# One buffer and one 1 MB transfer in place of two halves for two of three weight pieces

## The chip, the cores and the metric

The kernel runs on one core of one Trainium2 chip. The metric is the device time of one execution, in microseconds. The kernel before took 734.4 us (median of three runs, 733.27 to 735.97).

## The reference

Two decoder layers over 256 tokens of width 1024, in float32:

```
for l in 0, 1:
    x = LN(alpha*x + mixer_l(x))   # l=0: differential attention beside retention; l=1: forgetting attention
    h = LN(alpha*x + moe(x))       # router: 4 groups of 4 experts, top 2 of 16, FF = 512, silu(g)*u
    x = h + gate(h, p[l])          # per-layer input embedding, width 256
```

Every expert has three matrices (g and u of 1024 x 512, d of 512 x 1024). All 16 experts are computed for both layers.

## The kernel before

**Weights as pieces.** All weights lie in DRAM as 236 pieces of 1 MB, each 128 partitions by 2048 float32. `PLAN` lists them in the order of use: for layer 0, 16 pieces of the mixer (0 to 15), then 96 of experts and two "pp" pieces (half the size) of the MoE (16 to 113) and 4 "pg" pieces of the gate; layer 1 follows in the same way from 118, with its mixer up to 133 and its MoE from 134. A matrix g, u or d of one expert is two pieces, written here as d(l, e, fh): layer, expert, half.

**Buffers.** `fetch` takes the next piece of PLAN, asks the pool `wp` for room, and starts the transfers on SP's DMA queue (`dma_start`, line 289). The pool has 36 buffers of 128 x 1024 (512 KB, a row of 4 KB in each partition), so a piece has two of them and comes in two transfers. A buffer's next transfer is held back until the last reader of what lay in it is done. A few pieces (`PLACES`) go to other memory, among them three "late" ones and the ones in slots per layer: they come in one transfer of 1 MB. The pieces d(l, 10, 1) and d(l, 11, 1) come in transfers of 256 KB, so that the first of their rows can start early. SP executes its instructions strictly in order: a transfer that waits for its buffer holds back all that stand behind it. A transfer also waits for the one eight places ahead of it to have landed, since eight semaphores go round.

**The MoE.** Experts run in 7 units: pairs, one unit of four (12 to 15), and last the pair (10, 11), called LAST. For a unit, PE computes g and u (line 1309), transposes the product, and runs the down rows (line 1339). Matmul rows of a pair have 64 partitions each and two run side by side; those of the unit of four have 32.

**The end of layer 1.** In PLAN the tail of the last MoE reads d(1, 10, 0), d(1, 11, 0) (227, 228), three pg pieces (229 to 231, `EARLY`), d(1, 10, 1), d(1, 11, 1) (232, 233), the pp piece 234 and the pg piece 235. `early` (lines 401 to 408) splits the three EARLY pieces into high and low parts, which lie in 12 more buffers of the pool (tiles "wf"). After the last down rows come a layer norm, and the gate with its pg and pp weights (line 1553).

The order of instructions on each engine is set ahead by a scheduler from the program and the buffers' release; it needn't be the order in which the code asks.

Of the kernel before, what the change touches and what calls it, by code (L numbers as in the profile page):

```python
# [10 lines left out]
F32 = mybir.dt.float32  # L11
FR = mybir.dt.float32r
# [19 lines left out]
DEPTH = 2  # L32
NBUF = 18
CUT = 2
NSPL = 4
PPAT = 5

# [33 lines left out]
def plan():  # L71
    out = []
    for l in range(DEPTH):
        if l == 0:
            cols = [0, 512, 1536, 1024, 2048, 2560]
            out += [("ein", c, kh) for c in cols for kh in range(2)]
        else:
            def qk(g):
                return [("oqk", g, kh) for kh in range(2)]

            def v(h):
                return [("ov", h, kh) for kh in range(2)]
            out += qk(0) + v(0) + qk(1) + v(1) + qk(2) + qk(3)
        out += [("wo", l, kh, nh) for kh in range(2) for nh in range(2)]
        out += moe_steps(l)
        out += [k for k in [("pg", l, nh, kh) for nh in range(2) for kh in range(2)] if k not in EARLY]
    return out


PLAN = plan()  # L90
# [140 lines left out]
def trunk(ctx: ExitStack, tc, w, xT_d, pT_d, prm_d, rows_d, rb_d, cst_d, e_d, dt_d, out):  # L231
# [4 lines left out]
    big = ctx.enter_context(tc.tile_pool(name="big", bufs=1))  # L236
    wp = ctx.enter_context(tc.tile_pool(name="wp", bufs=NBUF * CUT))
    wsp = ctx.enter_context(tc.tile_pool(name="wsp", bufs=NSPL))
    small = ctx.enter_context(tc.tile_pool(name="small", bufs=2))
# [9 lines left out]

    def room(n=4):  # L250

        return [wp.tile([128, 2048 // CUT], F32, name="wt", tag="wt") for _ in range(n * CUT // 4)]

    def quarters(t):
        return [x[:, j:j + 512] for x in t for j in range(0, x.shape[-1], 512)]
# [3 lines left out]
    def source(key, c):  # L259

        if key[0] in ("g", "u", "d") and key[2] >= FIXED:
            l = key[1]
            of = w[(l * NE + FIXED) * 6:(l + 1) * NE * 6].rearrange("(x j) p c -> x j p c", j=6)
            if callable(ranked[l]):
                ranked[l] = ranked[l]()
            return of[bass.ds(ranked[l][key[2] - FIXED], 1), "gud".index(key[0]) * 2 + key[3], :, c]
        return w[AT[key], :, c]

    def fetch(n=1):
        for _ in range(n):  # L270
            i = pos[0]
            if i >= NCHUNK:
                return
            place = PLACE.get(i)
            if place == "split":
                t = [wsp.tile([128, 512], F32, name="wt", tag=g) for g in ("whi", "wlo") for _ in range(2)]
            elif place is None:
                t = room(2 if PLAN[i][0] == "pp" else 4)
            elif place == "late":
                t = [late[0].tile([128, 2048], F32, name="wt", tag="late")]  # L280
            else:
                t = [slot(XSLOT[PLAN[i][1]][place], "wt", shape=(128, 2048))]
            c = 0
            for part in t:
                n = part.shape[-1]

                m = 512 if PLAN[i][0] == "d" and PLAN[i][2] in UNITS[LAST] and PLAN[i][3] else n
                for j in range(0, n, m):
                    nc.sync.dma_start(out=part[:, j:j + m], in_=source(PLAN[i], slice(c + j, c + j + m)))
                c += n  # L290
            t = quarters(t)
            ahead[PLAN[i]] = t
            pos[0] += 1

    def take(key, drop=True):

        while key not in ahead:
            fetch()
        return ahead.pop(key) if drop else ahead[key]
# [5 lines left out]
    def slot(i, name, dt=F32, shape=(128, 8, S)):  # L305

        return big.tile(list(shape), dt, name=name, tag=f"s{i}")
# [18 lines left out]
    for k in range(8):  # L326
# [3 lines left out]
        c = (k % 4) * 512  # L330
# [19 lines left out]
    wf = prm[:, P_WF:P_WF + 256].rearrange("p (k e) -> p k e", k=8)  # L350
# [29 lines left out]
    def split(hi, lo, src, after=None, eng=None, first=None):  # L380
        with tc.issue_after(first.ins) if first else ExitStack():
            i = ACT.activation(hi, src, AF.Copy)  # L382
        with tc.issue_after(after.ins) if after else ExitStack():
            return i, (eng or DVE).tensor_tensor(lo, src, hi, op=OP.subtract)  # L384
# [10 lines left out]

    def prepare(keys, n=NSPL):

        for i in range(n):
            part(keys[i // 4], i % 4)

    def early(keys, after):

        for key in keys:
            for j in range(4):
                t = wp.tile([128, 2048 // CUT], FR, name="wf", tag="wt")
                hi, lo = t[:, 0:512], t[:, 512:1024]
                after = split(hi, lo, take(key, drop=j == 3)[j], after[1], None, after[0])
                parted[key, j] = hi, lo
        return after
# [219 lines left out]
    def even(x2, y2, acc):  # L629
        with ExitStack() as es:  # L630
# [23 lines left out]
            heads_T(kaT, 512, 1.0)  # L654
            centred(0)
            fetch(2)
            nc.sync.dma_start(out=scr, in_=bt)
            fetch()
# [965 lines left out]
```

## Time and profile before

| | before |
|---|---|
| median of three runs | 734.4 us |
| profiled execution, its own time | 737.25 us |
| its span | 735.4 us |
| PE busy | 711.4 us (97%) |
| DMA moved | 250.82 MB, mean 341 GB/s |
| mean granted TensorE clock | 0.995 |

The profiled execution took 2.85 us more than the median of the runs; sums of durations are held against its own span. The span is cut by the program into the mixer of layer 0 (to about 132 us), its MoE (to about 335), the mixer of layer 1 (to about 494), its MoE (to about 702), and the last norm and gate. "Busy" of PE contains rows that stretch because operands come late, so 97% is not a share of useful work.

### The profile page before, as it was taken

What the parts mean: (1) busy time and instruction counts of PE and PEld (TensorE: products, weight loads), DVE (VectorE), ACT (ScalarE), POOL (GpSimd) and SP (SyncE); (2) the same over time, 40 slices, a digit from 0 to 9 for tenths busy, and PEclk for the clock granted to TensorE, in tenths of its full rate; (3) what the DMA queues carried; (4) which work ended last, traced back from release to release, by engine and by line L of the source; (5) the groups of instructions that cost most, each with busy time, mean ns of one, the idle gap of its engine ahead of it and who ended that gap; (6) DMA issues with size and microseconds to landing.
All of it is one profiled execution on the core that took longest, in us unless ns stands there. A gap on an engine that the chain in (4) does not pass through costs nothing.

```text
span 735.4 us, 11580 instructions
## 1 busy us (share of the span) xinstructions
PE 711.4 (97%) x4126; PEld 427.8 (58%) x4126; DVE 320.7 (44%) x805; ACT 242.4 (33%) x507; POOL 45.8 (6%) x44
## 2 busy tenths in 40 slices
PE   6999999999999998999999999989999999999897
PEld 6977887434335334338989898764353343343267
DVE  6687776412103103019857666672031121120585
ACT  5557656201102001006667566561010110110441
POOL 3000111000000000004000000010000000000036
PEclk9999999999999999999999999999999999999899
DMA  8999977999999999999997337559999999999901
GB/s 287 354 410 408 371 263 261 322 389 415 410 408 414 408 407 410 408 377 401 409 408 301 128 141 282 185 189 333 412 413 409 412 411 408 406 410 408 391 4 58
DMA packets 70397, 250.82 MB, mean 341 GB/s; under 512 B 7835, under 2 KB 9408, under 8 KB 67648
## 3 DMA queue, kind: packets, MB, share of 16 engines
q1 hardware_dynamic: 70176, 249.51, 87.6%
q8 instruction: 34, 0.56, 0.3%
q0 software_dynamic: 160, 0.52, 0.2%
q14 instruction: 27, 0.22, 0.1%
HBM read 248.95 MB, written 1.05 MB: 340 GB/s over the span
## 4 chain that ended last, share of the span: by engine, by line
PE 76%; DMA 18%; DVE 3%; ACT 2%; issue 1%; POOL 0%; SPq 0%; DVEq 0%; ACTq 0%; POOLq 0%
PE w L1309 21%; DMA wt<-in_w_dram 18%; PE acc L420 13%; PE acc L434 13%; PE w L1339 11%; PE w L1247 3%; PE acc L1553 2%; PE acc L1359 2%; PE w L962 1%; PE w L1008 1%; PE w L1322 1%; PE w L1553 1%; DVE lnst L458 1%; PE w L622 1%; PE w L782 1%
## 5 line engine op out<-in xcount | busy, mean ns | idle before, releaser
L1309 PE MATMUL w<-wt,xg 128*64 128x512 f32 (+1 forms) x1024 | 202.7, 595 | 2.3 <-DMA wt<-in_w_dram 1.3
L1309 PEld LDWEIGHTS w<-wt,xg 128*64 128x64 f32 (+1 forms) x1024 | 63.7, 130 | 122.7 <-issue 112.6
L1339 PE MATMUL w<-wt,aT 128*64 128x512 f32 (+1 forms) x512 | 123.5, 604 | 3.7 <-DMA wt<-in_w_dram 3.5
L384 DVE TENSOR_TENSOR wlo<-wt,whi 128x512 fp32r<-128x512 f32 x145 | 106.3, 749 | 43.2 <-ACT whi L382 36.6
L382 ACT ACTIVATE whi<-wt 128x512 fp32r<-128x512 f32 x148 | 91.0, 629 | 65.6 <-PE acc L434 27.5
L1339 PEld LDWEIGHTS w<-wt,aT 128*64 128x64 f32 (+1 forms) x512 | 38.4, 132 | 80.1 <-issue 68.5
L1350 ACT ACTIVATE whi<-w,gg 128x512 fp32r<-128x512 f32 x28 | 19.3, 688 | 157.6 <-PE w L1339 150.4
L1316 DVE TENSOR_TENSOR a<-a,w 128x512 f32<-128x512 f32 x14 | 9.6, 688 | 127.2 <-PE w L1309 127.2
L434 PE MATMUL acc<-xh,whi 128*128 128x256 f32 x192 | 51.5, 293 | 5.6 <-ACT whi L382 5.6
L434 PE MATMUL acc<-xh,wlo 128*128 128x256 f32 x192 | 51.1, 290 | 0.0
L1315 ACT ACTIVATE a<-w 128x512 f32<-128x512 f32 x14 | 8.4, 597 | 123.0 <-PE w L1274 57.5
L1351 DVE SCALAR_TENSOR_TENSOR wlo<-w,gg,whi 128x512 fp32r<-128x512 f32 x28 | 20.6, 746 | 64.7 <-ACT whi L1350 64.4
L434 PEld LDWEIGHTS acc<-xh,whi 128*128 128x128 f32 x192 | 37.9, 199 | 6.8 <-ACT whi L382 6.6
L434 PEld LDWEIGHTS acc<-xh,wlo 128*128 128x128 f32 x192 | 38.0, 198 | 0.4 <-DVE wlo L384 0.2
L420 PE MATMUL acc<-whi,xh 128*128 128x512 f32 x96 | 38.1, 396 | 0.0
L420 PE MATMUL acc<-whi,xl 128*128 128x512 f32 x96 | 38.0, 396 | 0.0
L434 PE MATMUL acc<-xl,whi 128*128 128x256 f32 x192 | 37.5, 288 | 0.0
L420 PE MATMUL acc<-wlo,xh 128*128 128x512 f32 x96 | 37.1, 390 | 0.0
L1257 ACT ACTIVATE xg<-w,prm 128x256 f32<-128x256 f32 (+1 forms) x32 | 15.5, 533 | 62.9 <-PE w L1247 62.9
L1247 PE MATMUL w<-sel,n 128*128 128x256 f16 (+1 forms) x256 | 28.1, 260 | 2.6 <-ACT xg L1257 1.8
L434 PEld LDWEIGHTS acc<-xl,whi 128*128 128x128 f32 x192 | 29.9, 198 | 0.0
L1324 DVE COPY aT<-w 128x512 f32<-128x512 f32 x14 | 9.7, 690 | 45.7 <-PE w L1339 32.3
(318 smaller groups left out, 988.0 us busy)
## 6 DMA issues: line engine op xcount, KB each, us to landing
wt<-in_w_dram SPq DMA_DIRECT2D x406, 512.0 KB, 10.1
wt<-in_w_dram SPq DMA_DIRECT2D x21, 1024.0 KB, 9.3
wt<-in_w_dram SPq DMA_DIRECT2D x40, 256.0 KB, 5.8
x<-in_xT_dram SPq DMA_DIRECT2D x3, 256.0 KB, 5.4
dt<-in_dt_dram SPq DMA_DIRECT2D x1, 512.0 KB
tmp<-scr SPq DMA_DIRECT2D x1, 512.0 KB, 7.1
pT<-in_pT_dram POOLq DMA_DIRECT2D x2, 256.0 KB, 6.8
out_dram<-wt SPq DMA_DIRECT2D x2, 256.0 KB, 2.7
```

The costliest lines, as they stand in the source:

```text
L382: i = ACT.activation(hi, src, AF.Copy)
L384: return i, (eng or DVE).tensor_tensor(lo, src, hi, op=OP.subtract)
L420: PE.matmul(o, lhsT=wa[p], rhs=wb[q], start=start and i == 0, stop=stop and i == 2, skip_group_check=True)
L434: m = PE.matmul(outs[b], lhsT=ws[kk][i % 2][:, b * 128:(b + 1) * 128], rhs=x2[i // 2][:, kk, :], start=kk == 0 and b in first and i == 0, ...
L1247: PE.matmul(os[kb][:, b, :], lhsT=n2[j][:, tt, k * 128:(k + 1) * 128], rhs=sel[:, tt, 0:n], start=b == 0 and i == 0, stop=i == 3, skip_gro ...
L1257: ACT.activation(xt[:, k, 0:n], o[:, b, :], AF.Identity, bias=be, scale=g)
L1309: PE.matmul(o[m * i:m * i + m, :], lhsT=xg[p // 2][:, k, c:c + m], rhs=ws[i, k // 4][k % 4], start=k == 0, stop=k == 7)
L1339: PE.matmul(ob[nh][m * i:m * i + m, :], lhsT=aT[p][:, f, m * i:m * i + m], rhs=ws[i, f // 2][2 * (f % 2) + nh], start=f == 0, stop=f == 3)
L1350: last[:] = (ACT.activation(yh, ob[nh], AF.Copy, scale=gg), DVE.scalar_tensor_tensor(yl, ob[nh], gg, yh, op0=OP.mult, op1=OP.subtract))
L1351: DVE.scalar_tensor_tensor(yl, ob[nh], gg, yh, op0=OP.mult, op1=OP.subtract))
L1359: j = PE.matmul(acc[tt][nh], lhsT=sT[p // 2][:, p % 2, tt * 128:(tt + 1) * 128], rhs=y2[nh][i], start=False, stop=p == LAST and i == 1, sk ...
L1553: PE.matmul(gs[j], lhsT=h22[i % 2][:, kk, tt * 128:(tt + 1) * 128], rhs=ws[kk][i // 2][:, units[nh][j][1]], start=kk == 0 and i == 0, stop ...
```

## The change

Of the 36 half buffers, 24 are put together to 12 whole buffers of 128 x 2048 (1 MB, rows of 8 KB, tag "wb"); 12 halves stay. The memory is the same. A counter sends the pieces that go to the pool, but for the pp ones, to a half pair, a whole, a whole, and so on. A piece in a whole buffer comes in one transfer. The three EARLY pieces' parts lie in 6 whole buffers where they took 12 halves.

```diff
 NBUF = 18
 CUT = 2
+WHOLE = 12
...
     def room(n=4):
-        return [wp.tile([128, 2048 // CUT], F32, name="wt", tag="wt") for _ in range(n * CUT // 4)]
+        return [wp.tile([128, 2048 // CUT], F32, name="wt", tag="wt", bufs=(NBUF - WHOLE) * CUT) for _ in range(n * CUT // 4)]
+
+    def whole_room(name="wt", dt=F32):
+        return wp.tile([128, 2048], dt, name=name, tag="wb", bufs=WHOLE)
+
+    turn = [0]
...
+            elif place is None and PLAN[i][0] == "pp":
+                t = room(2)
             elif place is None:
-                t = room(2 if PLAN[i][0] == "pp" else 4)
+                turn[0] += 1
+                t = [whole_room()] if turn[0] * WHOLE % NBUF < WHOLE else room()
...
             for j in range(4):
-                t = wp.tile([128, 2048 // CUT], FR, name="wf", tag="wt")
-                hi, lo = t[:, 0:512], t[:, 512:1024]
+                if j % 2 == 0:
+                    t = whole_room("wf", FR)
+                hi, lo = [t[:, c:c + 512] for c in range(j % 2 * 1024, j % 2 * 1024 + 1024, 512)]
```

The order of SP's transfers at the end of the last MoE, before. Of the tiles, 6320 and 6321 are piece 231 (pg), 6335 and 6336 piece 232, 6341 and 6342 piece 233, 6381 the pp piece 234, 6458 and 6459 the pg piece 235. An "ISA" row is a wait for a buffer.

```order
L289 DMA wt_6320<-in_w_dram 128x1024
L289 DMA wt_6321<-in_w_dram 128x1024
L289 ISA
L289 DMA wt_6335<-in_w_dram 128x512
L289 ISA
L289 DMA wt_6335<-in_w_dram 128x512
L289 ISA
L289 DMA wt_6336<-in_w_dram 128x512
...
L289 DMA wt_6381<-in_w_dram 128x1024
L289 DMA wt_6458<-in_w_dram 128x1024
L289 DMA wt_6459<-in_w_dram 128x1024
```

And after, at the same place: 6049 and 6050 are piece 231, 6037 is piece 230, 6106 the pp piece 234, 6183 and 6184 the pg piece 235, 6062 piece 232 and 6067 piece 233. The line is 299 now.

```order
L299 DMA wt_6049<-in_w_dram 128x1024
L299 DMA wt_6050<-in_w_dram 128x1024
L299 DMA wt_6037<-in_w_dram 128x2048
L299 DMA wt_6106<-in_w_dram 128x1024
L299 DMA wt_6183<-in_w_dram 128x1024
L299 DMA wt_6184<-in_w_dram 128x1024
L299 ISA
L299 DMA wt_6062<-in_w_dram 128x512
...
L299 ISA
L299 DMA wt_6067<-in_w_dram 128x512
```

The pieces 234 and 235 (1.5 MB) stand ahead of the last two down pieces, where they stood behind them. Six whole buffers hold the parts of the EARLY pieces, and the whole buffer of piece 232 is that which d(1, 12, 1) leaves.

The second place is SP at the start of the mixer of layer 1, where before all pieces came in PLAN's order in pairs of halves. After the change 3167 is piece 118, 3346, 3408, 3554, 3624 and 3763 are pieces 120, 121, 123, 124 and 126, and 3263 and 3264 are piece 119:

```order
L299 DMA wt_3167<-in_w_dram 128x2048
L299 DMA wt_3346<-in_w_dram 128x2048
L299 DMA wt_3408<-in_w_dram 128x2048
L299 DMA wt_3554<-in_w_dram 128x2048
L299 DMA wt_3624<-in_w_dram 128x2048
L299 DMA wt_3763<-in_w_dram 128x2048
L299 DMA wt_3263<-in_w_dram 128x1024
L299 DMA wt_3264<-in_w_dram 128x1024
```

Whole pieces run ahead of the half pieces there; piece 119 comes five pieces later than PLAN has it. PE's order moves little: the rows are the same, with some down rows of experts 8 and 9 in larger groups.

## Rows read from the trace of the kernel before

**Rows 1.** This is the page: the span, PE's busy time, two lines of the span cut into 40 slices of 18.4 us (the granted clock in tenths, and GB/s), the count of DMA packets, and the chain that ended last, by engine.
```profile
span 735.4 us, 11580 instructions
...
PE 711.4 (97%) x4126; PEld 427.8 (58%) x4126; DVE 320.7 (44%) x805; ACT 242.4 (33%) x507; POOL 45.8 (6%) x44
...
PEclk9999999999999999999999999999999999999899
...
GB/s 287 354 410 408 371 263 261 322 389 415 410 408 414 408 407 410 408 377 401 409 408 301 128 141 282 185 189 333 412 413 409 412 411 408 406 410 408 391 4 58
DMA packets 70397, 250.82 MB, mean 341 GB/s; under 512 B 7835, under 2 KB 9408, under 8 KB 67648
...
PE 76%; DMA 18%; DVE 3%; ACT 2%; issue 1%; POOL 0%; SPq 0%; DVEq 0%; ACTq 0%; POOLq 0%
```

**Rows 2.** Windows of core 0, one row for a stretch: the stretch and its length in us, then busy time of PE, PEld, DVE, ACT and POOL (instructions), the granted clock, the DMA share and GB/s. The first two are the MoE of layer 0, the next two the mixer of layer 1, the last two the MoE of layer 1.
```profile
144.00:300.00 156.00, 152.78 (x809) 61.98 (x806) 29.74 (x69) 16.15 (x28) 0.74 (x1) 1.00 1.02 407
300.00:331.00 31.00, 30.61 (x146) 10.24 (x142) 3.01 (x6) 2.45 (x4) 0.00 (x0) 1.00 1.01 390
340.00:430.00 90.00, 89.48 (x668) 82.28 (x666) 62.92 (x137) 57.42 (x115) 3.92 (x4) 1.00 0.81 313
430.00:494.00 64.00, 62.03 (x455) 51.41 (x455) 44.10 (x163) 38.54 (x102) 3.36 (x4) 1.00 0.58 206
510.00:640.00 130.00, 128.74 (x695) 51.06 (x692) 22.81 (x51) 13.38 (x23) 0.58 (x1) 1.00 1.02 409
640.00:691.00 51.00, 47.56 (x230) 19.00 (x227) 14.16 (x27) 11.96 (x21) 0.00 (x0) 1.00 1.03 408
```

**Rows 3.** What PE waited for between 132 and 340 us (first two rows) and between 490 and 702 us (the third): line, releaser, us in total, times, longest.
```profile
PE w L1309 <- DMA wt<-in_w_dram: 0.6, 1, 0.6
...
PE w L1339 <- DMA wt<-in_w_dram: 0.3, 1, 0.3
...
PE w L1339 <- DMA wt<-in_w_dram: 3.2, 1, 3.2
```

**Rows 4.** PE's timeline in the MoE of layer 0: start, us, line, tiles, instructions, and in brackets the idle time ahead with what ended it. The first two rows are the first experts, the others the gate rows of the unit of four experts and the down rows of the last two units.
```profile
137.99 3.65 PE L1309 MATMUL w<-wt,xg 128*64 128x512 f32 x16
...
255.69 13.94 PE L1309 MATMUL w<-wt,xg 128*32 128x512 f32 x128 [0.62 <-DMA wt<-in_w_dram]
...
310.56 5.37 PE L1339 MATMUL w<-wt,aT 128*32 128x512 f32 x40
316.19 3.62 PE L1339 MATMUL w<-wt,aT 128*32 128x512 f32 x20 [0.27 <-DMA wt<-in_w_dram]
...
323.19 8.11 PE L1339 MATMUL w<-wt,aT 128*64 128x512 f32 x30
```

**Rows 5.** This is the page, DMA issues: transfers of weights by size, count, KB each, and median us from issue to landing.
```profile
wt<-in_w_dram SPq DMA_DIRECT2D x406, 512.0 KB, 10.1
wt<-in_w_dram SPq DMA_DIRECT2D x21, 1024.0 KB, 9.3
wt<-in_w_dram SPq DMA_DIRECT2D x40, 256.0 KB, 5.8
```

**Rows 6.** Windows again, columns as in rows 2. In the first and second stretch three transfers of 1024 KB land; the others hold transfers of 512 KB alone.
```profile
172.00:177.00 5.00, 4.96 (x39) 3.80 (x37) 2.63 (x6) 1.02 (x2) 0.00 (x0) 1.00 1.01 420
...
535.00:539.00 4.00, 4.00 (x34) 3.25 (x34) 1.51 (x4) 1.05 (x3) 0.00 (x0) 1.00 1.02 424
545.00:550.00 5.00, 5.00 (x32) 2.31 (x30) 0.91 (x3) 0.60 (x1) 0.00 (x0) 1.00 1.03 413
...
640.00:680.00 40.00, 39.10 (x205) 16.01 (x203) 6.50 (x15) 5.03 (x10) 0.00 (x0) 1.00 1.03 409
```

**Rows 7.** What SP's DMA queue waited for, columns as in rows 3: first the whole span, then 132 to 155 us, then 480 to 510 us; and after them windows of the start of either MoE, columns as in rows 2.
```profile
SPq L289 <- DMA wt<-in_w_dram: 248.4, 314, 2.0
...
SPq L289 <- PE w L1309: 18.0, 9, 7.0
...
SPq L289 <- PE w L1309: 18.3, 7, 9.5
...
137.00:152.00 15.00, 15.00 (x78) 5.96 (x77) 2.60 (x6) 2.90 (x4) 0.00 (x0) 1.00 1.00 344
...
505.00:510.00 5.00, 5.00 (x26) 1.65 (x24) 0.00 (x0) 1.47 (x2) 0.00 (x0) 1.00 0.95 316
```

**Rows 8.** This is the chain that ended last, from 682 us (start, us, what); PE's timeline of the last down rows; windows there, columns as in rows 2.
```profile
682.22 9.54 DMA wt<-in_w_dram
691.81 8.40 PE w L1339 x16
...
684.02 4.56 PE L1339 MATMUL w<-wt,aT 128*64 128x512 f32 x14
691.81 8.39 PE L1339 MATMUL w<-wt,aT 128*64 128x512 f32 x16 [3.22 <-DMA wt<-in_w_dram]
...
688.00:691.00 3.00, 0.58 (x2) 0.00 (x0) 3.00 (x5) 2.68 (x5) 0.00 (x0) 1.00 1.03 392
691.00:694.00 3.00, 2.19 (x3) 0.75 (x4) 2.05 (x4) 1.15 (x2) 0.00 (x0) 0.51 1.04 384
694.00:698.00 4.00, 4.00 (x10) 1.22 (x9) 0.00 (x0) 0.00 (x0) 0.00 (x0) 0.52 1.02 386
698.00:702.00 4.00, 3.86 (x14) 1.58 (x11) 1.50 (x2) 1.37 (x2) 0.00 (x0) 1.00 0.14 54
```
## The prediction, made before the changed kernel ran

> **What bounds the kernel now.** I read the page first. PE is busy 97% of the span, and the chain that ended last is 76% PE and 18% DMA. In the slices, GB/s stands near 410 in two long stretches and falls to 128 to 333 between them and to almost nothing at the end, while the granted clock is 9 tenths or more in every slice but one near the end [rows 1]. So there are stretches with different limits, and I cut them with windows [rows 2]. In both MoE stretches the DMA share is 1.01 to 1.03 at about 409 GB/s: the weight stream is full there. In the mixer of layer 1 it falls to 0.81 and 0.58; PE sets the pace in that stretch.
>
> PE's waits seem to deny a DMA limit: 0.9 us in the whole first MoE, 3.2 us at the end of the second [rows 3]. But the rows themselves stretch. Rows of 32 partitions take 13.94 / 128 = 0.109 us each when their weights are there, and the down rows of the unit of four take (5.37 + 3.62) / 60 = 0.150: 2.5 us over. Rows of 64 partitions take 3.65 / 16 = 0.228, and the last 30 take 8.11, which is 1.3 us over [rows 4]. So the stream holds PE at the end of the first MoE by 0.3 + 2.5 + 1.3 = 4.1 us. At the end of the second the chain passes from a DMA of 9.54 us straight to the last 16 down rows [rows 8]. Before these ends, PE has a stock of pieces in the ring and eats it up. A change of the stream's rate is therefore worth something at the two ends only, where all that it gained before is paid at once.
>
> **Part one: the rate of the stream.** The page counts 70397 packets, and those of 8 KB or more number 70397 - 67648 = 2749, about 21 x 128 [rows 1, 5]. So each partition's row of a transfer is one packet, and the change halves the packets of whole pieces. What an 8 KB row is worth shows where three of the 21 transfers of 1 MB land: 420 and 424 GB/s, beside 413 and 409 where only halves land [rows 6]. A piece of 1.049 MB takes 2.564 us at 409 and 2.497 at 420: 0.07 us less. The ends are 0.04 (413 against 420) and 0.09 (409 against 424). In the full stretches lie 63 pool pieces in layer 0 (pieces 40 to 110) and 67 in layer 1 (158 to 231), of which two thirds, 42 and 44, become whole. This gives -2.9 us and -3.1 us, together -6.0 (from -3.4 to -7.7). Both lie below what PE could take up: 4.1 us in layer 0, and in layer 1 the wait of 3.2 us and the stretched rows behind it.
>
> The Trainium skill ("DMA: Bandwidth & Descriptors", section "Why small descriptors are slow (HBM only)") charges a fixed three cycles per packet beside one per 32 bytes. By that a row of 4 KB would cost 131 cycles and one of 8 KB 259, an estimate of 1.2% where the windows show 2.7%. It is the smaller gain among the rivals below.
>
> **Part two: a whole buffer comes free later, and is filled later.** Each MoE starts with the ring full: SP waits there for PE's line 1309, 18.0 us in one and 18.3 in the other, and the stream runs at 344 and 316 GB/s though its share reads about 1 [rows 7]. Sixteen rows of line 1309 read two pieces in 3.65 us; a first half is free 1.8 us before its second [rows 4]. With whole buffers the first transfers of the stream start up to 1.8 us later; where the next piece is a half pair, nothing is lost. I take the middle, 0.9 us in layer 0 and 0.8 in layer 1 (0 to 1.8 each), since one of three pieces is still a pair.
>
> The other side of this is at PE: half a piece can't be used before the rest has landed. In the middle of the stream the stock hides it. At the end of the first MoE PE waits for a half of the unit of four (the 0.27 us before the row at 316.19 [rows 4]); half a piece is 2.564 / 2 = 1.28 us, so 0 to 1.3 us later, and I take 0.9, since two of three pieces are whole. In layer 1 the pieces at the same place come through the same ring, but what is lost there is inside the wait that follows.
>
> Eight transfers in flight are now up to 8 MB rather than 4. SP's waits for an earlier transfer (248.4 us, 314 times [rows 7]) lessen. In full stretches that gives nothing, since the 16 engines have work at any time; in the starts, where buffers are short, nothing either. I cost it at 0, from -2.5 us (15 us at 344 rather than 409 GB/s [rows 7]) up to 0.
>
> **Part three: the order at the end of layer 1.** Pieces 234 and 235, 1.5 MB, now go ahead of the last two down pieces: 1.5 x 2.56 = 3.85 us later for 232 and 233. Before, PE ended its last row of 227 and 228 at 684.02 + 4.56 = 688.58 and waited 3.22 us to 691.81 [rows 8]. The stream reaches this place 3.1 - 0.8 = 2.3 us sooner, so the wait would end at 691.81 - 2.3 + 3.85 = 693.4: 4.8 us of waiting rather than 3.2. Nothing gained falls back on anything else, because PE's other work of the MoE is done; behind the late pieces only the layer norm and the gate wait, and the gate's own weights now land earlier.
>
> What follows the wait runs slowly already. PE idles from 688.6, the granted clock is 0.51 and 0.52 from 691 to 698 (the lower of its two levels, 1.2 GHz), and 1.00 after 698; the 16 rows take 8.39 us where they would need 16 x 0.228 = 3.65 [rows 4, 8]. I assume that these 8.39 us only shift. The ends: if the level rises again at 698 as now, each us of later start costs only half of it, so the 3.85 are worth 1.9; if the low level lasts on over the rows behind, more (first rival).
>
> **Part four: the rest, at nothing.** In the mixer of layer 1 the half pairs fall behind the whole pieces: 119 comes up to five pieces later, 5 x 2.56 = 12.8 us. PE waits for no DMA in that mixer, the stream has room in it (313 and 206 GB/s [rows 2]), and pieces there land well ahead of their rows; by my reading of when buffers come free, 119 still lands some 8 us before its rows start. If that cover were gone, 12.8 us at most less the 8. The six whole buffers for the EARLY parts hold the same bytes as 12 halves. The shifted down rows of experts 8 and 9 leave PE the same work.
>
> **The sum.** Layer 0: -2.9 + 0.9 + 0.9 = -1.1. Layer 1: -3.1 + 0.8 + 3.85 = +1.55. Together +0.45 us. The profiled execution's span of 735.4 becomes 735.85, its time 737.25 becomes 737.7. It is 2.85 us over the median of the runs, so for runs I say 734.4 + 0.45, or 734.9 us. With every term at its better end but the queue (-7.7 + 0 + 0 + 1.9) the sum is -5.8, with every one at its worse (-3.4 + 1.8 + 1.8 + 1.3 + 3.85) it is +5.3; near -4 and +4.5 is what I take as likely.
>
> **Rivals.**
> First, slower: the longer wait keeps PE's clock low for longer. The wait is 4.8 us rather than 3.2, and PE then idles again in the layer norm right behind its last rows. If the level that now returns at 698 [rows 8] returned only after all of the late rows, those behind the 16, about 3.5 us of scatter and gate rows, would double. That is +3.5 on top of +0.45, or 738.4 us. For it: 16 rows already run from first to last at the low level but for two us. Against it: the clock has come back in about 7 us once, with the same rows. It decides if the low rows reach past 702.
>
> Second, faster: the reorder is hidden. If the clock comes back at 698 the later start costs 1.9 rather than 3.85; the losses at the restart are nil because half pairs stand first, and a deeper queue fills part of the starts, -1.4. The sum is -6.0 + 1.9 - 1.4 = -5.5, or 728.9 us. For it: eight transfers of 1 MB are in flight in place of eight of half. Against it: at these starts SP waits for PE's buffers and not for landings [rows 7].
>
> Third, the change doesn't do what it says: an 8 KB row is worth less than the windows of three transfers suggest; they are 4 and 5 us long, and a piece more or less landing at their edge is 2%. By half the gain per piece, the sum is +0.45 + 3.0 = +3.5, 737.9 us. With no gain at all, +6.5, or 740.9 us.
> By the Trainium skill's three cycles per packet ("DMA: Bandwidth & Descriptors", "Why small descriptors are slow (HBM only)"), 86 whole pieces would give an estimate of -2.5 us in place of -6.0, and so 738.4 us; the trace has no stretch of whole pieces alone that would settle it.
>
> **How the numbers follow.** What a measurement of this kernel can tell from no change is about 0.5%, 3.7 us. My forecast with its neighbourhood has 0.58, the first rival 0.13, the second 0.15, the third 0.14. Of the forecast most lies within 3.7 us of no change. The second rival lies beyond it on the faster side, and a little of the forecast does: faster 0.18. The first rival and half of the third lie at or past it on the slower side: slower 0.21. Same 0.61. The range from 730.0 to 739.5 leaves out the far half of the second rival and the far end of the third.
>
> **What would show it.** In the changed profile: packets under 8 KB fall by some 40%; windows in the full stretches read 417 to 421 GB/s; the row that now starts at 316.19 starts about 1 us earlier relative to the start of the span; SP's transfers of 232 and 233 stand last and PE waits 4 to 5 us for them; the granted clock is near 0.5 for some 7 us from there. The prediction is wrong if the rate stays at 409 (third rival), if the low clock reaches into the gate (first), if PE waits 3 us or less at the end (second), or if PE waits for a weight in the mixer of layer 1.

## The result, and the profile after

The changed kernel takes 738.59 us (median of eight runs, 736.22 to 739.38); the kernel before, run beside it, takes 734.63. The ratio is 1.0051 with an interval of 1.0040 to 1.0062, or 3.7 us more (2.9 to 4.6). The forecast was 0.45 us more, 734.9 us, in a range of 730.0 to 739.5.

The traces tell another story at first sight: this is the page of the changed kernel (PEclk and GB/s in 40 slices).

```profile
span 734.6 us, 11119 instructions
...
PE 706.2 (96%) x4126; PEld 424.7 (58%) x4126; DVE 321.5 (44%) x805; ACT 241.6 (33%) x507; POOL 46.3 (6%) x44
...
PEclk9999999999999999999999999999999999999999
...
GB/s 269 386 418 415 249 329 265 298 404 419 418 415 420 414 414 416 418 407 419 413 363 173 229 122 308 158 216 333 407 420 415 418 418 414 415 416 418 348 1 58
DMA packets 51242, 250.78 MB, mean 341 GB/s; under 512 B 5707, under 2 KB 7280, under 8 KB 31472
```

Its span is 734.6 us, 0.8 less than that of the trace of before [rows 1]. But it is the fastest of the eight executions (736.22 us in all), and the trace of before, with 737.25, lay above all three runs shown with it. Two single traces of a kernel whose executions differ by 3 us can't be subtracted to find 3.7 us. They show where time goes; the ratios of the medians say how much it is.

The packets under 8 KB fell from 67648 to 31472, by 53% where the prediction said some 40%. The windows in the same stretches as [rows 2, 6, 7] (columns as in rows 2):

```profile
144.00:300.00 156.00, 152.87 (x824) 62.50 (x822) 30.21 (x73) 17.97 (x30) 0.74 (x1) 1.00 1.02 414
300.00:331.00 31.00, 30.13 (x138) 9.72 (x134) 3.45 (x5) 2.77 (x5) 0.00 (x0) 1.00 1.02 411
510.00:640.00 130.00, 128.80 (x700) 51.39 (x697) 23.54 (x53) 13.39 (x23) 0.58 (x1) 1.00 1.02 415
640.00:680.00 40.00, 38.88 (x203) 15.29 (x200) 7.55 (x16) 6.00 (x11) 0.00 (x0) 1.00 1.02 416
...
137.00:152.00 15.00, 15.00 (x84) 6.64 (x84) 3.00 (x8) 2.90 (x4) 0.00 (x0) 1.00 0.92 331
```

The full stretches read 414 to 416 GB/s, where [rows 2, 6] had 407 to 409, and 411 against 390 at the end of the first MoE, where 390 is the lowest of four traces with halves (the kernel before twice, and two edits below that leave this part alone: 390, 404, 403 and 397 from 300 to 330 us). At the start of that MoE 331 stands where [rows 7] has 344; a later run whose program is the same up to there reads 345, so this one number shows nothing. The transfers on the page (size, count, KB each, us to landing):

```profile
wt<-in_w_dram SPq DMA_DIRECT2D x154, 1024.0 KB, 13.7
wt<-in_w_dram SPq DMA_DIRECT2D x140, 512.0 KB, 13.1
```

154 transfers carry 1 MB. Each is under way for 13.7 us where [rows 5] had 10.1 for a half. The halves too take 13.1 us now, so it isn't their own size: more lies in the queue, and they wait there. PE's timeline at the ends of both MoE stretches (columns as in [rows 4]):

```profile
308.02 6.23 PE L1350 MATMUL w<-wt,aT 128*32 128x512 f32 x40
314.97 3.62 PE L1350 MATMUL w<-wt,aT 128*32 128x512 f32 x20 [0.72 <-DMA wt<-in_w_dram]
...
322.09 8.11 PE L1350 MATMUL w<-wt,aT 128*64 128x512 f32 x30
```

```profile
682.22 4.56 PE L1350 MATMUL w<-wt,aT 128*64 128x512 f32 x14
692.01 6.96 PE L1350 MATMUL w<-wt,aT 128*64 128x512 f32 x16 [5.23 <-DMA wt<-in_w_dram]
```

The rows of the unit of four start their last part at 314.97 rather than 316.19 [rows 4], after a wait of 0.72 rather than 0.27 us. At the end PE waits 5.23 us rather than 3.22 [rows 8]. The chain (start, us, what) goes from one transfer to the next to that point. Those in the full stretch last 15 us rather than 10, and the last one 12:

```profile
664.92 14.95 DMA wt<-in_w_dram
...
680.00 11.97 DMA wt<-in_w_dram
...
692.01 6.98 PE w L1350 x16
```

And the windows around the wait:

```profile
688.00:692.00 4.00, 0.00 (x0) 0.00 (x0) 3.88 (x7) 3.72 (x8) 0.00 (x0) 0.97 1.03 396
692.00:694.00 2.00, 1.99 (x3) 0.74 (x4) 1.02 (x2) 0.00 (x0) 0.00 (x0) 0.50 1.05 386
694.00:696.00 2.00, 2.00 (x6) 0.63 (x7) 0.00 (x0) 0.00 (x0) 0.00 (x0) 0.71 0.73 268
696.00:698.00 2.00, 2.00 (x9) 0.65 (x6) 0.00 (x0) 0.00 (x0) 0.00 (x0) 1.00 0.01 3
```

The granted clock is 0.50 when the last rows start, and 1.00 again before 696. In the trace of before it stayed at 0.51 and 0.52 to 698 [rows 8]. So the drop (the stretch at the lower level) lasted 7 us in that execution and 3.4 in this one.

### The profile page after: what moved, and what is told of

It reads as the page before. It is cut to its first block, busy times and chain, and to the rows that moved or that the text cites. A ratio compares the mean times of both kernels' runs of the same rounds, so it can differ in the third digit from the quotient of the medians.

```text
span 734.6 us, 11119 instructions
## 1 busy us (share of the span) xinstructions
PE 706.2 (96%) x4126; PEld 424.7 (58%) x4126; DVE 321.5 (44%) x805; ACT 241.6 (33%) x507; POOL 46.3 (6%) x44
## 2 busy tenths in 40 slices
DMA packets 51242, 250.78 MB, mean 341 GB/s; under 512 B 5707, under 2 KB 7280, under 8 KB 31472
## 5 line engine op out<-in xcount | busy, mean ns | idle before, releaser
L1350 PE MATMUL w<-wt,aT 128*64 128x512 f32 (+1 forms) x512 | 120.9, 599 | 6.6 <-DMA wt<-in_w_dram 6.6
L394 DVE TENSOR_TENSOR wlo<-wt,whi 128x512 fp32r<-128x512 f32 x145 | 107.0, 754 | 43.6 <-ACT whi L392 38.3
L1258 PEld LDWEIGHTS <-n 128*128 128x128 f16 x256 | 22.0, 98 | 9.4 <-issue 6.3
## 6 DMA issues: line engine op xcount, KB each, us to landing
wt<-in_w_dram SPq DMA_DIRECT2D x154, 1024.0 KB, 13.7
wt<-in_w_dram SPq DMA_DIRECT2D x140, 512.0 KB, 13.1
```

What stands on the lines that cost most here:

```text
L1258: PE.matmul(os[kb][:, b, :], lhsT=n2[j][:, tt, k * 128:(k + 1) * 128], rhs=sel[:, tt, 0:n], start=b == 0 and i == 0, stop=i == 3, skip_gro ...
L1350: PE.matmul(ob[nh][m * i:m * i + m, :], lhsT=aT[p][:, f, m * i:m * i + m], rhs=ws[i, f // 2][2 * (f % 2) + nh], start=f == 0, stop=f == 3)
```

## The experiments

Every ratio is to the kernel before, run beside the edited one; a thousandth is 0.735 us. Two edited kernels are compared by their ratios, with the bounds that the ends of both intervals give. A row is one matmul instruction of the trace; one matmul of the code shows as two.

**The kernel before once more.** No edit.

> The kernel before, unchanged. All theories: ratio 1.000 (within 0.2%), around 734.6 us. Its profile is wanted from the chip on which the edits run: the trace shown so far was 2.6 us above the median of its kernel, while the changed kernel's trace was 2.4 us below its own. If profiles are fair samples, this one shows a wait of about 3.2 us ahead of the last 16 down rows and a stretch of about 7 us at the lower clock.

734.48 us, ratio 0.9998 (0.9987 to 1.0010). Its trace, with a span of 732.5 us, is a better base than the first. PE's timeline of the last down rows, then windows:

```profile
682.58 4.56 PE L1339 MATMUL w<-wt,aT 128*64 128x512 f32 x14
690.21 7.09 PE L1339 MATMUL w<-wt,aT 128*64 128x512 f32 x16 [3.07 <-DMA wt<-in_w_dram]
```

```profile
690.00:692.00 2.00, 1.79 (x3) 0.62 (x4) 1.47 (x3) 0.67 (x2) 0.00 (x0) 0.62 1.03 378
692.00:694.00 2.00, 2.00 (x4) 0.52 (x4) 0.00 (x0) 0.00 (x0) 0.00 (x0) 0.52 1.00 346
694.00:696.00 2.00, 2.00 (x10) 0.75 (x7) 0.00 (x0) 0.00 (x0) 0.00 (x0) 1.00 1.01 399
```

The wait is 3.07 us, as before, and the clock is back by 694, some four microseconds sooner than in [rows 8]. The mean granted clock of the executions of the kernel before has a median of 0.997, with 0.995 as the lowest; the trace that the prediction read was such a lowest one (0.995). The changed kernel's executions have 0.994 to 0.996. A thousandth of the mean is 735 x 0.001 / 0.5, or 1.5 us more at the lower level; by the medians, 0.997 and 0.995, an execution of the changed kernel has some 3 us more of it. Seven of its eight executions have 0.994 or 0.995, as the trace with the drop of 7 us had; the profiled one, 0.996, is the odd one, so its short drop doesn't stand for the kernel.

**The last two down pieces back in their place.** In the changed kernel:

```diff
+            elif place is None and i in (232, 233):
+                t = room()
             elif place is None:
                 turn[0] += 1
```

The two pieces lie in halves again and go out ahead of 234 and 235. As the counter passes them over, piece 235, the last, falls to a whole buffer: there are 155 transfers of 1 MB rather than 154.

> The changed kernel, but pieces 232 and 233 lie in half buffers, so that they go out again ahead of 234 and 235 (pp and pg). Theory A (the order at the end costs 3.85 us, and the 8 KB rows pay for the rest): 3 to 4 us below the changed kernel, about 735 us, ratio 1.000. Rival C (what costs is that whole buffers come free late and fill late; the order at the end is hidden): no gain, about 738.5 us, ratio 1.005. Rival B (8 KB rows are worth nothing in most executions, the order costs all): about 734.6 us, ratio 1.000, as in A.

732.61 us, ratio 0.9975 (0.9963 to 0.9987). Against the changed kernel's ratio this is 0.0076 or 5.6 us less (by the ends of both intervals 3.9 to 7.3), and it is faster than before. Theory A's direction holds and rival C falls. The size is more than the 3.85 us of A. Timeline and windows:

```profile
688.42 6.36 PE L1352 MATMUL w<-wt,aT 128*64 128x512 f32 x16 [1.39 <-DMA wt<-in_w_dram]
```

```profile
688.00:690.00 2.00, 1.58 (x4) 0.59 (x5) 1.63 (x3) 2.00 (x5) 0.00 (x0) 1.00 1.05 386
690.00:692.00 2.00, 2.00 (x7) 0.68 (x6) 2.00 (x5) 1.98 (x4) 0.00 (x0) 1.00 1.07 398
```

The wait is 1.39 us, 3.84 less than in the changed kernel: the 1.5 MB. That it fits to the hundredth is luck, since the same wait is 1.36 and 1.58 us in two sister kernels below. What comes on top fits the clock, which another run tests below. The clock stays at 1.00 here, and the 16 rows take 6.36 us, so 3.65, which the prediction had worked out for them, was too little: row by row, the eight of the first expert start alone, and those of the second only when its piece lands, 2.7 us later in this trace; one expert's rows follow each other every 0.43 us.

**The order alone, in the kernel before.** In PLAN:

```diff
 PLAN = plan()
+PLAN = PLAN[:232] + PLAN[234:] + PLAN[232:234]
```

> The kernel before, all halves, with PLAN's last four pieces in the changed kernel's order: 234 and 235 ahead of 232 and 233. Theory A: the wait ahead of the last 16 down rows grows by 3.85 us from 3.2 to about 7, and the time with it: 738.4 us, ratio 1.005. Rival: the clock comes back at the same time and hides half: 736.5 us, ratio 1.0025. Rival C (the order is hidden): 734.6 us, ratio 1.000.

739.78 us, ratio 1.0066 (1.0048 to 1.0084), 4.8 us more.

```profile
683.52 4.56 PE L1340 MATMUL w<-wt,aT 128*64 128x512 f32 x14
695.13 7.12 PE L1340 MATMUL w<-wt,aT 128*64 128x512 f32 x16 [7.04 <-DMA wt<-in_w_dram]
```

```profile
692.00:694.00 2.00, 0.00 (x0) 0.00 (x0) 0.55 (x1) 0.00 (x0) 0.00 (x0) 0.50 1.03 388
...
696.00:698.00 2.00, 2.00 (x4) 0.69 (x3) 0.00 (x0) 0.00 (x0) 0.00 (x0) 0.50 0.69 255
698.00:700.00 2.00, 2.00 (x9) 0.60 (x8) 0.00 (x0) 0.00 (x0) 0.00 (x0) 0.84 0.09 32
```

The wait grew from 3.07 to 7.04 us, by 3.97 where 3.85 were worked out. All the halves and 4 KB rows are as before, so the loss of the order is shown by itself. The clock rival (half hidden) falls: nothing is hidden.

**4 KB rows in whole buffers.** In the changed kernel's `fetch`:

```diff
-                m = 512 if PLAN[i][0] == "d" and PLAN[i][2] in UNITS[LAST] and PLAN[i][3] else n
+                m = 512 if PLAN[i][0] == "d" and PLAN[i][2] in UNITS[LAST] and PLAN[i][3] else (1024 if place is None else n)
```

> The changed kernel with its 12 whole buffers and its order, but each whole piece comes in two transfers with rows of 4 KB. Theory A: the 6.0 us of the stream are lost, 738.6 + 6 = 744.6 us, ratio 1.0135 (from 1.010 to 1.016), and the windows in the full stretches read 409 GB/s. Rival B (8 KB rows are worth nothing): as the changed kernel, 738.6 us, ratio 1.005. Rival C: as A.

742.78 us, ratio 1.0100 (1.0081 to 1.0119). Rival B falls: 8 KB rows are worth 0.0049 or 3.6 us (1.4 to 5.8 by the ends of the intervals), less than the 6.0 of theory A. The edit also halves the size of a transfer and what lies in the queue, so "8 KB rows" stands here for longer rows and larger transfers together; no run tells them apart. The windows of the full stretches go back (the changed kernel's first, for comparison), and at the end the clock stays low for longest:

```profile
152.00:300.00 148.00, 144.87 (x788) 59.89 (x786) 29.32 (x70) 16.17 (x28) 0.74 (x1) 1.00 1.02 417
...
152.00:300.00 148.00, 144.77 (x772) 59.29 (x770) 29.05 (x68) 15.56 (x27) 0.74 (x1) 1.00 1.02 410
510.00:640.00 130.00, 128.74 (x693) 50.96 (x690) 22.81 (x51) 13.38 (x23) 0.58 (x1) 1.00 1.02 407
```

```profile
694.00:696.00 2.00, 0.00 (x0) 0.00 (x0) 1.94 (x4) 1.80 (x4) 0.00 (x0) 0.60 1.00 396
...
704.00:706.00 2.00, 2.00 (x8) 0.70 (x5) 0.00 (x0) 0.00 (x0) 0.00 (x0) 0.84 0.00 0
```

**Whole buffers alone.** The edit before this, together with the last two down pieces in halves.

> Whole buffers alone: each whole piece in two transfers with 4 KB rows, and the last two down pieces in halves, in the old place. Against the kernel before only the grain of the buffers is changed. Theory A (late freeing at the start of either MoE and the start of the program cost 2.6 to 3 us): 737.4 us on a base of 734.6, ratio 1.004. Rival (the grain costs nothing, and the 8 KB rows pay only as far as the last kernels are faster than before, 2 us): ratio 1.000.

738.50 us, ratio 1.0042 (1.0028 to 1.0056): 3.1 us for the grain of the buffers (their larger size), as theory A had it. The order at the end, from this kernel to the one before it, is 0.0058 or 4.3 us (1.8 to 6.7), a third measure of it. And 8 KB rows, from this kernel to the one with the last pieces back in their place, are 0.0067 or 4.9 us (3.0 to 6.8). Where the grain costs shows against the traces of halves; here the second trace of before, its window at the start of the first MoE, and its rows of the unit of four:

```profile
137.00:152.00 15.00, 15.00 (x78) 6.01 (x77) 2.59 (x6) 2.90 (x4) 0.00 (x0) 1.00 0.99 355
```

```profile
310.61 7.84 PE L1339 MATMUL w<-wt,aT 128*32 128x512 f32 x60
```

And the same of the kernel with whole buffers and 4 KB rows:

```profile
137.00:152.00 15.00, 15.00 (x81) 6.38 (x81) 2.59 (x6) 2.90 (x4) 0.00 (x0) 1.00 0.95 326
```

```profile
311.17 5.43 PE L1352 MATMUL w<-wt,aT 128*32 128x512 f32 x40
317.26 3.62 PE L1352 MATMUL w<-wt,aT 128*32 128x512 f32 x20 [0.66 <-DMA wt<-in_w_dram]
```

The stream starts at 326 rather than 355 GB/s over 15 us; 355 is the highest of four traces with halves (344, 355, 344, 348), so it falls 0.3 to 0.4 MB behind, 0.7 to 1.1 us. Part of that is due to PE, whose expert rows start 0.56 us later (132.66 against 132.10). The rows of the unit of four end at 320.9, with a wait of 0.66 us, where those four traces have 318.5 to 319.8. In the second MoE, PE needs 200.1 us from the first expert rows to the last 16 down rows where it needed 197.6. The two traces differ by 5.0 us in span, more than the 3.1 of the ratios, so these stages show the places and not the exact shares.

The price of the grain depends on the rows. From 5 us before PE's first expert rows to 25 us after, the stream reads 337 to 344 GB/s in layer 0 and 263 to 276 in layer 1 with halves, 322 and 323, and 237 and 239 with whole buffers and 4 KB rows, but 335 to 336 and 249 to 262 in the three traces with the changed kernel's buffers and 8 KB rows. So with 8 KB rows more than half of the loss at the starts comes back: some 3.4 us of stream (18 and 29 GB/s less over 30 us each) become some 1.4 (5 and 14 less), where the prediction had 1.7 (0.9 + 0.8). The 3.1 us are the grain at 4 KB rows.

**PE kept busy in the wait.** In the changed kernel, between the first 16 and the last 16 of the last down rows:

```diff
                 for f, nh, i in steps:
-                            PE.matmul(ob[nh][m * i:m * i + m, :], lhsT=aT[p][:, f, m * i:m * i + m],
+                            if p == LAST and l == DEPTH - 1 and (f, nh, i) == (2, 0, 0):
+                                idle = bank("w")
+                                for _ in range(5):
+                                    with tc.issue_after(j.ins):
+                                        j = PE.matmul(idle, lhsT=aT[p][:, 0, :], rhs=ws[0, 0][0],
+                                                      start=True, stop=True)
+                            j = PE.matmul(ob[nh][m * i:m * i + m, :], lhsT=aT[p][:, f, m * i:m * i + m],
...
```

> The changed kernel, with five matmuls of no use (128 columns by 512, into a bank that nobody reads) between the first 16 and the last 16 of the last down rows, so that PE works some 4.3 of the 5.2 us of the wait. Theory D (the idle wait brings the lower clock, and the lower clock costs on top of the wait): granted clock 1.00 through the last rows, 2 us less, 736.6 us, ratio 1.003. Rival E (the last rows are paced by their eight transfers of 256 KB, 2 MB at 409 GB/s or 5.1 us, and the clock costs under 0.7 us): 738 to 738.6 us, ratio 1.005. Rival F (the clock falls all the same): no change, and 0.50 to 0.52 in the windows.

736.83 us, ratio 1.0024 (1.0010 to 1.0037): 0.0027 or 2.0 us less than the changed kernel (0.2 to 3.8 by the ends of the intervals). Theory D holds; E and F fall.

```profile
687.37 4.56 PE L1354 MATMUL w<-wt,aT 128*128 128x512 f32 x10
692.81 6.33 PE L1356 MATMUL w<-wt,aT 128*64 128x512 f32 x16 [0.87 <-DMA wt<-in_w_dram]
```

```profile
692.00:694.00 2.00, 1.19 (x3) 0.46 (x4) 1.83 (x4) 0.53 (x2) 0.00 (x0) 1.00 1.04 383
694.00:696.00 2.00, 2.00 (x8) 0.65 (x6) 0.00 (x0) 0.00 (x0) 0.00 (x0) 1.00 0.71 264
```

The added matmuls (ten rows) take 4.56 us, the clock stays at 1.00, and the last 16 rows take 6.33 us. The mean clock of its executions is 0.998 to 1.000. In these two traces the rows end at the same time (699.14 here, 698.97 in the changed kernel): the 2 us stand in the ratios alone, since the changed kernel's trace is its shortest, and its short drop ends just as the second expert's rows start (695.3).

**The same in the kernel before**, with three such matmuls.

> The kernel before, with three matmuls of no use in the wait ahead of the last 16 down rows (2.6 of some 3.1 us). It asks how much of the time before is the lower clock. Theory D (the clock falls in a wait of 3 us too and costs there as well): granted clock 1.00, 0.5 to 1.5 us less than before, ratio 0.998 to 0.999. Rival (in most executions of the kernel before the lower clock is short or hidden by the last transfers): no change, ratio 1.000.

734.35 us, ratio 0.9995 (0.9985 to 1.0005): no change, so the rival holds.

```profile
687.48 2.84 PE L1343 MATMUL w<-wt,aT 128*128 128x512 f32 x6
690.73 6.35 PE L1345 MATMUL w<-wt,aT 128*64 128x512 f32 x16 [0.41 <-DMA wt<-in_w_dram]
```

```profile
690.00:692.00 2.00, 1.59 (x4) 0.46 (x4) 1.99 (x4) 1.15 (x2) 0.00 (x0) 1.00 1.05 389
692.00:694.00 2.00, 2.00 (x8) 0.67 (x6) 0.00 (x0) 0.00 (x0) 0.00 (x0) 1.00 1.05 382
```

The clock is 1.00, and the 16 rows take 6.35 us and end at 697.08; the second trace of before has 7.09 us and 697.30, with a clock of 0.52 up to 694. So a drop of some 3.5 us costs 0.7 us in the rows. That of the second trace falls on the first expert's rows, and these have time: the second expert's piece lands 3.2 us after the first row starts in that trace, and the rest of both runs side by side. Only a drop that lasts beyond that landing slows the end; in the first trace of before, where it lasts to 698, the 16 rows took 8.39 us [rows 8], 2.0 more than at full clock.

Time and clock do go together in the kernel before: of 89 of its executions the 27 with a mean of 0.998 or more took 734.1 us on average, the 53 with 0.996 or 0.997 took 735.3, and the 9 with 0.995 took 736.5. But PE kept busy, with 0.999 or 1.000 in every execution, wins only 0.4 us (from 1.1 won to 0.4 lost). So most of that difference isn't the price of the clock; an execution with a longer wait may have both.

**The first pieces in two transfers.** To the kernel with the last pieces in their place, whole pieces among the first six come in two:

```diff
-... else n
+... else (1024 if i < 6 else n)
```

> The kernel with pieces 232 and 233 in halves, and besides the whole pieces among the first six (3 and 4) come in two transfers each. In the changed kernel's trace PE falls 1.2 us behind between 17 and 21 us, where piece 3 comes whole. Theory (half of a first piece is used before the rest is there): PE's first expert rows start 0.7 to 1.2 us earlier, near 132.0, and the time falls by as much against the 732.6 us of the kernel without it: 731.6 us, ratio 0.996. Rival (the stock in the ring gives it back by the end of the first MoE, where the stream decides): the start is earlier, the time the same, 732.6 us, ratio 0.9975.

732.69 us, ratio 0.9965 (0.9951 to 0.9979), which can't be told from 0.9975, nor from 0.996. PE's first expert rows start at 132.59 us, against 132.77 without the edit, 132.10 in the second trace of before, and 133.25 in the changed kernel. So the start decides, and both failed: it didn't come back to 132.0, so nothing could be given back later either. The kernel with 4 KB rows throughout starts at 132.66, so it isn't the single transfer of piece 3 that sets it back. Nor is it the share of whole buffers: with 15 of them (below) PE starts at 132.07 and 131.58. What sets it back is open. In the eight traces with 12 whole buffers the rows start at 132.5 to 133.4, in the four with halves at 131.7 to 132.2.

**The late down pieces of layer 0 in two transfers**, on top of that.

```diff
-... else (1024 if i < 6 else n)
+... else (1024 if i < 6 or PLAN[i][0] == "d" and PLAN[i][1] == 0 and PLAN[i][2] >= 10 else n)
```

> As the first of this set, and the down pieces of experts 10 to 15 in layer 0 that are whole come in two transfers of half the size. Theory (in the changed kernel PE waits there for a whole piece where it used a half before): 0.5 to 0.9 us less than the first of this set, 730.9 us, ratio 0.995. Rival (the rows are paced by the stream's rate, and 4 KB rows take 0.06 us more for each of some 8 pieces): 0 to 0.5 us more than the first of this set.

732.13 us, ratio 0.9960 (0.9945 to 0.9974). The difference is within the intervals. In the traces the first MoE ends at 328.74 rather than 329.99, but its wait of the last rows ends at 689.26 rather than 689.05; the gain of 1.2 us is seen there and not at the end. Inconclusive.

**15 whole buffers and 6 halves**, on top of the edit of the first pieces: `WHOLE = 15`.

> As the first of this set with 15 whole buffers and 6 halves, so that five of six pieces come whole. Theory (the stream's rate counts at the two ends): 22 more whole pieces in the full stretches by 0.06 us, 1.3 us less, 730.3 us, ratio 0.994. Rival (late freeing and late filling grow with the share of whole buffers): 0.9 us for each MoE more, 732.5 us or above, ratio 0.9975 or above.

732.44 us, ratio 0.9959 (0.9947 to 0.9972). Neither ratio was met, and the trace shows why.

```profile
681.10 10.00 PE L1352 MATMUL w<-wt,aT 128*64 128x512 f32 x30
694.71 1.22 PE L1372 MATMUL acc<-whi,sT 128*128 128x512 f32 x2 [3.62 <-ACT whi L1363]
```

The last down rows end at 691.10, 4.3 us before those of its sister with 12 wholes, the kernel with the first pieces in two transfers (695.40). Then PE idles 3.62 us for ACT: the third early pg piece now lands behind the down pieces, and ACT splits it first. The clock falls in this wait too, to 0.50 from 694 to 701, and the eight pp rows behind it take 4.87 us rather than 3.59.

**Two versions with only two early pg pieces** (the third comes behind the last down pieces), one on the 12 whole buffers with both edits of transfers, one on the 15:

```diff
-EARLY = [("pg", DEPTH - 1, 0, 0), ("pg", DEPTH - 1, 0, 1), ("pg", DEPTH - 1, 1, 0)]
+EARLY = [("pg", DEPTH - 1, 0, 0), ("pg", DEPTH - 1, 0, 1)]
```

> A version meant to beat both: the changed kernel with the last two down pieces in halves, the first pieces and the late down pieces of layer 0 in two transfers, and only two pg pieces ahead of the last down pieces; the third comes behind them. The wait ahead of the last 16 down rows has 1 MB less before it, 2.5 us: theory 1.4 us of wait are gone and the rest is hidden, 730.8 us, ratio 0.994. Rival (the third pg piece is then split on the path of the gate): 732 to 734 us, ratio 0.996 to 0.999.

> The kernel with 15 whole buffers, the last two down pieces in halves and the first pieces in two transfers, and only two pg pieces early. In its sister with three, ACT had the scatter's operands ready 3.6 us late, behind the split of the third pg piece. Theory: this wait goes, 3 us less than its sister, 729.4 us, ratio 0.992. Rival (the split of the second pg piece takes its place): ratio 0.996, as its sister.

With 12: 732.57 us, ratio 0.9963 (0.9948 to 0.9979), no gain over its sister (0.9960), as the rival had it: its down rows end 2.1 us sooner (693.44 against 695.57), and the gate's rows then wait for DVE, which splits the third pg piece, to 721.8. With 15: 730.00 us, ratio 0.9932 (0.9914 to 0.9950), faster than the kernel before by 0.5 to 0.9% and the best of all; against its sister it is 2.0 us, though the ends of the two intervals just overlap. Its timeline:

```profile
680.22 9.96 PE L1352 MATMUL w<-wt,aT 128*64 128x512 f32 x30
690.14 1.37 PE L1372 MATMUL acc<-whi,sT 128*128 128x512 f32 x3
```

The scatter rows follow the down rows at once: the 3.62 us of ACT are gone, and the clock stays at 1.00.

## Why the prediction was right and wrong

The time lies in the range, which was 9.5 us wide, but 3.3 us above the forecast of +0.45. The prediction was right in what moves and in which direction, and wrong in two sizes, in one assumption, and in a stage that it left out. Nearly all errors go the same way, so the range held by its width and not because they cancelled.

Added up from runs that change one thing each, the sum is +3.1 (grain) - 4.9 (8 KB rows) + 5.6 (order at the end) = +3.8 us, with 3.7 measured. That it comes out proves nothing: the three are the steps of one path from the kernel before to the changed one, so their sum is the measured ratio by construction. Each has an uncertainty of one to two microseconds, and along other paths 8 KB rows are 3.6 and the order 4.8 or 4.3.

The traces give a sum that is independent of the ratios. In the first column are the means of the four traces with halves (the kernel before twice, the order alone, PE kept busy), in the second of the three with the changed kernel's order (the kernel itself, PE kept busy, last pieces back in place). From the last line the two traces with the other order at the end (the order alone, and the last pieces back in place) are left out.

| us | halves | changed | difference | forecast |
|---|---|---|---|---|
| start of the program to the first expert rows | 132.0 | 133.0 | +0.9 | nothing said |
| from there to the last down row of layer 0 | 198.5 | 197.0 | -1.5 | -1.1 |
| from there, over the mixer, to the first expert rows of layer 1 | 162.66 | 162.99 | +0.3 | 0 |
| from there to the end of the wait ahead of the last 16 down rows | 197.7 | 199.5 | +1.7 | +1.55 |

Single traces of a column lie within 1.4 us of each other. Both MoE stretches came out near the forecast. These four give +1.4 us; what follows the wait depends on the drop: 41.6 to 42.0 us to the end without one (three traces), 42.3 with the short one of the second trace of before, 43.6 with the long one of the first. If the changed kernel's usual execution has the long one, as its mean clock suggests, and that of the kernel before the short one, that is up to 1.3 us more. Of the 3.7 us (2.9 to 4.6) about one stays without a place.

- **The rate of the stream, -6.0 us.** With 4 KB rows in the same buffers the rate falls back, so the gain is that of longer rows in larger transfers; which of the two gives it isn't shown. Measured are 3.6 and 4.9 us. The windows give 2.5 us in the first full stretch (148 us, 410 to 417 GB/s) and 2.5 in the second (174 us, 409 to 415), 5.0 together, 0.06 us a piece and not 0.07. The term was read from windows of 4 and 5 us; its lower end would have been nearer to 3.6, though not to 4.9. One reading behind it doesn't hold: the 30 rows that took 8.11 us, "1.3 us over", take 8.11 in every trace here, whatever the stream does, so at the end of the first MoE the stream held PE by 2.8 us and not by 4.1. The third rival had the right kind of error, and a fraction of its size.
  The Trainium skill's three cycles per packet ("DMA: Bandwidth & Descriptors", "Why small descriptors are slow (HBM only)") would, by an estimate, have moved 410 to about 413 GB/s with two thirds of the pieces whole. Here 417 were reached, so the measurement goes beyond the rule by a factor of two.
- **The grain of the buffers, +2.6 us in all** (0.9 + 0.9 + 0.8). Measured are 3.1 (2.1 to 4.1), with 4 KB rows. It shows where it was expected, in slower starts of the stream and in the rows of the unit of four; with 8 KB rows the starts lose less. The start of the program was left out of the sum, without a reason: PE is 0.9 us late there, and why stays open.
- **The order at the end, +3.85 us.** As a wait it was right: 3.97 us in one pair of traces, 3.84 in the other. As time it is 4.8, 5.6 and 4.3 us (each known to one or two). The step that failed is "I assume that these 8.39 us only shift". They were read in an execution with one of the longest drops of the clock, and were taken to be the cost of it at any time. In the kernel before the drop costs too little to be measured (0.9995 with PE kept busy, 0.7 us in the rows of its second trace), in the changed kernel 2.0 us (0.2 to 3.8). Its executions have some 3 us more at the lower level, and what lasts beyond the landing of the second piece is time in which rows take 0.85 us rather than 0.43. That a longer wait makes a longer drop agrees with the means (0.997 before, 0.993 to 0.995 with the order alone and 7 us of wait, 0.998 to 1.000 with 1.4 us of wait), but not with each trace: 5.23 us of wait had a drop of 3.4, and 3.22 us one of 7. What sets the length is open.
- **The first rival** said that the longer wait would cost clock, 738.4 us, and comes nearest to the time. It was right that the clock costs more; its place was wrong: in their traces the low clock does not reach into the rows behind the 16 in the changed kernel or in the kernel before with the changed order; it slows the 16 rows themselves. In the kernel with 4 KB rows in whole buffers, which waits 7.5 us, the low level does last to 705, but the 16 rows last to 707.
- **The second rival** needed the restart losses to vanish and the reorder to be hidden. Both are excluded. That the deeper queue filled the starts isn't seen: they are no faster than with halves, and a transfer stays longer in the queue.
- **The mixer of layer 1** cost next to nothing: PE takes 162.96 us from the end of the first MoE to the first expert rows of the second, against 162.68, and waits for no weight there.

Of the signs that the prediction named, the packets (53% fewer rather than 40), the rate (415 to 417, at the lower edge of 417 to 421), the row at 316.19 (1.2 us earlier), the last place of 232 and 233 and the wait of about 5 us came out. "Near 0.5 for some 7 us" didn't in the trace, though the mean clock of the other seven executions speaks for it.

## What to carry to other kernels

A larger transfer is bought with a larger buffer, and what it wins in rate is partly lost where buffers come free late; measure both, with the old transfer in the new buffer, before the change is judged, and mind that the price may not be the same with the new transfer in it. Give every stage a term, the start of the program too. When buffers are put into classes, look at the compiled order of the transfers: what decides may be a pair of late pieces that a full class pushes behind others. And a wait of some microseconds ahead of a matrix engine's last rows can cost more than itself, as the clock falls in it (here some 2 us on 5.2).

## What was not expected

- Matmuls of no use in a wait can win time: five of them in the 5.2 us wait of the changed kernel won 2.0 us (0.2 to 3.8), three in the 3.1 us wait of the kernel before nothing that can be measured.
- How long the clock stays low differs between executions of one kernel: to 698 in the first trace of before, to 694 in the second. With waits of 0.4 to 1.6 us ahead of the same rows (the kernels with PE kept busy, and those with the last pieces back in their place) it stayed at 1.00.
- A single trace was 2.6 us above its kernel's median and another 2.4 us below; the difference of the two had the wrong sign.
- Eight transfers in flight of up to 1 MB take 15 us to land in the full stretch, where eight halves take 10; the rate is 1.7% higher over the first full stretch (410 to 417 GB/s).
